# A two-layer encoder on one core: the attention's prologue in an order written by hand, pair 0's keys left unscaled, and x loaded into eight tiles of its own

## The chip, the cores and the metric

The kernel runs on one core of one Trainium2 chip. The metric is the device time of one execution in microseconds; a kernel's time is the median of several executions. The engines are named as in the profile: PE (matmuls), PEld (its weight loads), DVE, ACT, POOL, and SP, which here only issues transfers (DMAs).

## The reference, cut to what matters

The model has 512 tokens of width 1024 and two layers. Layer 0 mixes by stick-breaking attention (16 heads of 64), layer 1 by a gated linear recurrence; each is followed by an MLP with squared relu of width 4096, and a last RMS norm closes. All inputs and weights are float32. The change touches the attention and what is just behind it:

```python
h = rms_norm(x, norm_mix[0])
qkv = (h @ w_qkv).reshape(B, S, 3, 16, 64)
z = einsum('bhqd,bhkd->bhqk', q, k) * 64 ** -0.5        # per block of 128 queries
log_keep = where(mask, log_sigmoid(-z), 0)              # mask: k_pos < q_pos
after = reverse cumsum(log_keep) - log_keep
w = where(mask, exp(log_sigmoid(z) + after), 0)
o = einsum('bhqk,bhkd->bhqd', w, v)
x = x + o @ w_o
h = rms_norm(x, norm_mlp[0]);  u = relu(h @ w1);  x = x + (u * u) @ w2
```

## The kernel before, in words

**Layout.** x is held transposed, as 8 chunks of 128 channels by 512 tokens. A product of a weight with x is 8 steps over the chunks. Every float32 operand is cut into a high and a low half (`wh`, `wl` for weights: ACT casts the raw weights to the high half, L172, and DVE subtracts it from them, L173; `xgh`, `xgl` for x scaled by the norm's gain, `halves`, L110; `bh`, `bl` for the input of an output projection). One step is then three matmuls of 512 columns (`three`, L176 to L180). The RMS norm's factor depends on the token alone, so it is applied to the products: the sum of squares over the channels is gathered in one tile (ACT squares, POOL or DVE add).

**Who orders what.** Inside the attention the program order of PE is kept as written (`manual_schedule` for PE); the other engines' instructions, and SP's transfers, are put in order by the compiler's scheduler, from a simulated timeline. Every engine runs its own list in order, so an instruction that waits holds all that is behind it.

**The prologue (L267 to L303).** Ten warm-up matmuls run while the first data come. ACT's queue issues six fetches for the two weight slabs of pair 0 (q and k, each in parts of 2, 2 and 4 chunks), SP's queue the 8 chunks of x and the columns of gains. START is the order in which x chunks and slab parts are cut into halves, FIRST the order of the first 16 steps. The sum of squares is made by two chains of adds (even chunks on POOL, odd ones on DVE), which are added at L303.

**The norm (`inverse`, L305).** Four column sums on PE (L309, eight rows in the trace), a root on ACT, a reciprocal and the diagonal on DVE; then one product (L324) that spreads the factor over all partitions, as `r`. Its first part runs ahead of the filling steps, its second behind step BROAD = 4, and then pair 0's k is scaled with `r` and cut (`k_halves`, L247).

**The filling steps and the chains (L464 to L506).** The steps of the projections make up a list `fill`: for pair 1 its k, its q and the value projection of pairs 0 and 1, for pairs 2 to 7 k, q and half of a value projection (24 steps), at last the output projection: chunks 4 and 5 over their first 5 input chunks (EARLY; kept as `early`), chunks 0 to 3 over 7. Between them, at due times counted in filling steps, stand the steps of two chains of each pair p: 8 score steps from SCORE0 + PACE p (q times k into a bank `z`, two sigmoids on ACT, a mask on POOL, a scan on DVE, a product on POOL), and 17 value steps from VAL0 + PACE p (PE transposes the weights, L421, ACT and DVE cut them into `th` and `tl`, L434 and L435, PE multiplies with v; the last one writes `bh` and `bl` of the pair, L459 and L460).

To move halves of q and k to where the two heads need them, `stacked` (L226) issues four transfers for each of q, kh and kl. These read the tiles `xh` and `xl`, of which there is one each.

**Behind the chains (L509 to L542).** Chunks 0 to 3 get their last input chunk, the slabs of chunks 4 to 7 are loaded and cut, the 8 chunks of x are loaded anew into one tile `x`, POOL adds `early` to chunks 4 and 5, and `residual` finishes chunks 4 to 7, adds each chunk to x (L527), cuts it (L113, L114) and squares it for the next norm. The MLP's first product follows.

PSUM has eight banks, named by tags with two each: `acc`, `t`, `o`, `z`.

## Time and profile before

| | us |
|---|---|
| three executions | 1144.65, 1146.91, 1147.21 |
| median | 1146.91 |
| the profiled execution | 1143.47 |
| its span, first to last instruction | 1141.8 |
| attention and output projection, in that span | 0 to about 270 |

A profile shows one execution. A row of the timeline gives the start, the duration, the engine, the line, the operation and its operands, and in brackets how long the engine had been idle before it and what ended that. A row of the waits gives engine, line and what it waited for: the total, how often, the longest. Durations of single PE rows overlap, because matmuls are pipelined; what one costs is the distance of two starts.

### The profile page before, as it was taken

Reading aid. Unit: us, or ns where it says so; the run is one execution under the profiler, and the core shown is the slowest. Engines: PE = TensorE matmul, PEld = TensorE weight load, DVE = VectorE, ACT = ScalarE, POOL = GpSimd, SP = SyncE. Lnnn points to the kernel's source line nnn. Section 1 sums busy time; section 2 is a strip of 40 time slices with the busy share of each in tenths; the row PEclk is TensorE's granted clock in tenths of the full one; section 3 lists DMA queues with packets and bytes.
Section 4 is the critical chain, followed back from the end, with each engine's and each line's share of the span. In section 5 each row is a group of like instructions: output and inputs, shape, how many; then the busy total and the mean of one; then the engine's idle time right before and its main releaser. Section 6 shows DMA issues by size and latency. Waiting matters only on the chain.

```text
span 1141.8 us, 13730 instructions
## 1 busy us (share of the span) xinstructions
PE 1108.6 (97%) x5164; PEld 916.5 (80%) x5164; DVE 606.8 (53%) x741; ACT 464.9 (41%) x738; POOL 364.4 (32%) x328
## 2 busy tenths in 40 slices
PE   8899999989999999999999999799999999999997
PEld 6788888867888888888888788688888888888886
DVE  6477776738533443433464769855433433433513
ACT  6566666746322222221244457834222222222332
POOL 2345445425611520520543000422611511611520
PEclk9999999999999999999999999899999999999999
DMA  7544354316332332233232222122322332233401
GB/s 240 149 130 129 94 150 114 88 39 221 110 94 93 101 99 92 93 95 106 95 104 93 78 78 92 56 74 98 105 92 93 96 108 92 92 101 102 148 1 74
DMA packets 41154, 117.34 MB, mean 103 GB/s; under 512 B 7424, under 2 KB 8192, under 8 KB 41088
## 3 DMA queue, kind: packets, MB, share of 16 engines
q1 hardware_dynamic: 39904, 114.89, 32.4%
q10 hardware_dynamic: 1184, 1.57, 0.5%
q8 instruction: 41, 0.67, 0.3%
q14 instruction: 25, 0.20, 0.1%
HBM read 101.76 MB, written 2.10 MB: 91 GB/s over the span
## 4 chain that ended last, share of the span: by engine, by line
PE 86%; DVE 6%; ACT 4%; issue 2%; DMA 1%; POOL 1%; SPq 0%; ACTq 0%; DVEq 0%; POOLq 0%
PE ps_acc L178 10%; PE ps_acc L179 10%; PE ps_acc L180 10%; PE ps_t L179 7%; PE ps_t L178 7%; PE ps_t L180 7%; PE ps_o L179 7%; PE ps_o L180 7%; PE ps_o L178 7%; DVE wl L173 2%; PE ps_t L421 1%; PE ps_acc L342 1%; PE ps_acc L343 1%; PE ps_acc L344 1%; PE ps_o L443 1%
## 5 line engine op out<-in xcount | busy, mean ns | idle before, releaser
L172 ACT CAST wh<-raw 128x1024 fp32r<-128x1024 f32 (+3 forms) x206 | 185.7, 918 | 487.7 <-issue 217.8
L173 DVE TENSOR_TENSOR wl<-raw,wh 128x1024 fp32r<-128x1024 f32 (+3 forms) x206 | 259.6, 1272 | 61.2 <-ACT wh L172 60.3
L556 POOL TENSOR_TENSOR u<-t 128x512 f32<-128x512 f32 x64 | 66.5, 1041 | 403.9 <-DVE t L553 400.8
L178 PE MATMUL ps_acc<-xgh,wh 128*128 128x512 f32 x368 | 148.6, 404 | 0.8 <-ACT wh L155 0.8
L179 PE MATMUL ps_acc<-xgh,wl 128*128 128x512 f32 x368 | 146.0, 397 | 0.0
L180 PE MATMUL ps_acc<-xgl,wh 128*128 128x512 f32 x368 | 145.9, 396 | 0.0
L557 POOL TENSOR_TENSOR bl<-u,bh 128x512 fp32r<-128x512 f32 x64 | 131.4, 2054 | 8.6 <-issue 3.8
L178 PE MATMUL ps_t<-xgh,wh 128*128 128x512 f32 x224 | 88.3, 394 | 0.0
L179 PE MATMUL ps_t<-xgh,wl 128*128 128x512 f32 x224 | 88.0, 393 | 0.0
L180 PE MATMUL ps_t<-xgl,wh 128*128 128x512 f32 x224 | 87.7, 392 | 0.0
L180 PEld LDWEIGHTS ps_acc<-xgl,wh 128*128 128x128 f32 x368 | 70.2, 191 | 16.0 <-DVE xgl L114 0.4
L178 PEld LDWEIGHTS ps_acc<-xgh,wh 128*128 128x128 f32 x368 | 70.2, 191 | 14.9 <-ACT wh L155 1.1
L179 PEld LDWEIGHTS ps_acc<-xgh,wl 128*128 128x128 f32 x368 | 70.3, 191 | 13.3 <-DVE wl L156 0.5
L405 DVE TENSOR_TENSOR_SCAN scan<-keep,later 128x128 f32<-128x128 f32 (+1 forms) x64 | 60.1, 940 | 35.1 <-ACT keep L396 34.4
L178 PE MATMUL ps_acc<-bh,wh 128*128 128x512 f32 x190 | 75.0, 394 | 0.8 <-DVE x L527 0.8
L179 PE MATMUL ps_acc<-bh,wl 128*128 128x512 f32 x190 | 74.5, 392 | 0.0
L180 PE MATMUL ps_acc<-bl,wh 128*128 128x512 f32 x190 | 73.7, 391 | 0.0
L180 PE MATMUL ps_o<-xgl,wh 128*128 128x512 f32 x176 | 68.6, 391 | 1.0 <-DVE xgl L114 1.0
L179 PE MATMUL ps_o<-xgh,wl 128*128 128x512 f32 x176 | 69.5, 395 | 0.0
L178 PE MATMUL ps_t<-bh,wh 128*128 128x512 f32 x176 | 68.7, 391 | 0.5 <-ACT wh L172 0.5
L179 PE MATMUL ps_o<-bh,wl 128*128 128x512 f32 x176 | 69.2, 393 | 0.0
L178 PE MATMUL ps_o<-bh,wh 128*128 128x512 f32 x176 | 68.9, 391 | 0.0
(228 smaller groups left out, 2198.5 us busy)
## 6 DMA issues: line engine op xcount, KB each, us to landing
raw<-in_w_m SPq DMA_DIRECT2D x120, 512.0 KB, 3.5
raw<-in_w_in SPq DMA_DIRECT2D x16, 512.0 KB, 3.5
raw<-in_w_qk SPq DMA_DIRECT2D x14, 512.0 KB, 4.3
x<-in_xT SPq DMA_DIRECT2D x16, 256.0 KB, 5.7
raw<-in_w_v SPq DMA_DIRECT2D x8, 512.0 KB, 3.9
kl<-xl SPq DMA_DIRECT2D x32, 128.0 KB, 3.4
raw<-in_w_ro SPq DMA_DIRECT2D x8, 512.0 KB, 3.5
raw<-in_w_last SPq DMA_DIRECT2D x8, 512.0 KB, 4.2
```

What stands on the lines that cost most here:

```text
L172: A.copy(wh[:, k, :], raw[:, k, :])
L173: V.tensor_tensor(wl[:, k, :], raw[:, k, :], f(wh[:, k, :]), ALU.subtract)
L178: PE.matmul(ps, wh, ah, start=start, stop=False)
L179: PE.matmul(ps, wl, ah, start=False, stop=False)
L180: PE.matmul(ps, wh, al, start=False, stop=stop)
L342: PE.matmul(ps, xgh[:, k, ts], wh, start=k == 0, stop=False)
L343: PE.matmul(ps, xgh[:, k, ts], wl, start=False, stop=False)
L344: PE.matmul(ps, xgl[:, k, ts], wh, start=False, stop=k == C - 1)
L405: V.tensor_tensor_scan(sc[:, S - n : S][:, ::-1], keep[:, :n][:, ::-1], later[:, S - n :][:, ::-1], 1.0, ALU.mult, ALU.max,)
L421: PE.transpose(tr[:, (qb - kb) * P : (qb - kb + 1) * P], w[pair, j, qb][:, kb * P : (kb + 1) * P], ident,)
L556: G.tensor_tensor(u, t, t, ALU.mult)
L557: G.tensor_tensor(bl[:, c, :], u, f(bh[:, c, :]), ALU.subtract)
```

## The change

It does the following.

- **Prologue.** ACT, DVE, POOL and SP follow the program's order there. ACT's queue issues only four fetches, SP's queue the others: the last parts of q and k behind x chunk 4, then the slabs of pair 1 (`n`, `m`) and of the first value projection. START now lists the squares (`s`) and the cutting of `n` and `m` too. All eight squares have tiles of their own.
- **The norm.** Its two parts stand behind filling steps 4 (SUMS) and 8 (BROAD), with `high_priority` for ACT and DVE.
- **Pair 0.** Its k isn't scaled: both products are cut as soon as they are there (`first_halves`), and its scores are multiplied by `r` (DVE, PSUM to SBUF) before the sigmoids. All copies of it go out on SP's queue, head by head.
- **Pair 1** does q before k, from slabs cut in the prologue, in banks `t` and `o`. The first value slabs are cut behind the norm's root and its copy, and later slabs behind the copy.
- **Chains.** PACE is 23.7, VAL0 is 35, and the last pair's two chains span 4 steps less. The two sigmoids change places.
- **Output projection.** What is left of chunks 4 and 5 (3 input chunks, two of them here) and of 6 (7) are filling steps at the end of the list, with weight halves in tiles of the score halves (`late_slab`). Then each of chunks 0 to 6 gets its last input chunk.
- **x.** Eight tiles (`home`) hold the first x, then `keep`, `w3` and `osum`, and at last x again; seven of them are loaded when the late steps begin, where POOL adds `early` too.

Cut to its core:

```diff
 START = [
-    ("x", 0), ("q", 0), ("k", 0), ("x", 1), ("x", 2), ("q", 1), ("x", 3), ("k", 1),
-    ("x", 4), ("q", 2), ("x", 5), ("k", 2), ("x", 6), ("x", 7),
+    ("x", 0), ("q", 0), ("k", 0), ("s", 0), ("x", 1), ("q", 1), ("k", 1), ("x", 2), ("s", 1), ("x", 3),
+    ("s", 2), ("x", 4), ("q", 2), ("k", 2), ("x", 5), ("x", 6), ("x", 7), ("n", 0), ("n", 1), ("s", 3),
+    ("s", 4), ("s", 5), ("s", 6), ("s", 7), ("m", 0), ("m", 1),
 ]
-PACE = 24
+PACE = 23.7
-VAL0, VALS = 39, 21
-BROAD = 4
+VAL0, VALS = 35, 21
+LESS = 4
+SUMS = 4
+BROAD = 8
...
+    HOMES = (*(("keep", 4),) * 4, *(("w3", 3),) * 3, ("osum", 1))
...
+        def first_halves(pq, pk):
+            qh, ql = parted(pq, "x")
+            h = hp.tile([P, S], F32R, tag="th", name="th", bufs=3)
+            l = hp.tile([P, S], F32R, tag="tl", name="tl", bufs=3)
+            A.copy(h, pk)
+            V.tensor_tensor(l, pk, f(h), ALU.subtract)
+            q[0], kh[0], kl[0] = [], [], []
+            for j in range(2):
+                for tag, two, to in (("q", (qh, ql), q), ("kh", (h, h), kh), ("kl", (l, l), kl)):
+                    t = hp.tile([P, S], F32R, tag=f"{tag}{j}", name=f"{tag}{j}")
+                    for a, part in zip(half, two):
+                        nc.sync.dma_start(out=f(t[a, :]), in_=f(part[half[j], :]))
+                    to[0].append(t)
...
+        parts += [slab_parts(w, (0, 4, 8)) for w in (w_qk[0, 1], w_qk[1, 1], w_v[0, 0], w_v[0, 1])]
...
+        with tc.manual_schedule(engines=others):
+            for i in range(2):
+                for j in range(2):
+                    parts[j][2](i, A)
+            for c in range(C):
+                nc.sync.dma_start(out=xcs[c], in_=xT[:, c, :])
...
+                if c == 4:
+                    for j in range(2):
+                        parts[j][2](2)
+            for j in range(2, 6):
+                for i in range(2):
+                    parts[j][2](i)
+            for kind, c in START:
...
+                else:
+                    A.activation(sqs[c], xcs[c], AF.Square)
+                    if c > 1:
+                        e, acc = ((G, sums), (V, odd))[c % 2]
+                        e.tensor_tensor(acc, acc, sqs[c], ALU.add)
+            V.tensor_tensor(sums, sums, odd, ALU.add)
+            for i, k in FIRST:
+                xg_step(first[i], k, *parts[i][:2])
+            first_halves(*first)
...
+                    if pair == 0:
+                        V.tensor_tensor(keep[:, :n], z[:, :n], norm["r"][:, :n], ALU.mult)
+                        z = keep
+                    A.activation(wt, z[:, :n], AF.Sigmoid, scale=norm["rp"][:, qb : qb + 1])
                     A.activation(keep[:, :n], z[:, :n], AF.Sigmoid, scale=norm["rn"][:, qb : qb + 1])
-                    A.activation(wt, z[:, :n], AF.Sigmoid, scale=norm["rp"][:, qb : qb + 1])
...
+            if pair == 1:
+                return [
+                    (qk_steps(0, pair, q_halves, parts[2][:2], "t"), C),
+                    (qk_steps(1, pair, k_halves, parts[3][:2], "o"), C),
+                ]
...
+        LATE = sum(n for _, n in fill)
+        fill += [(so_late(4, "t", EARLY), 2), (so_late(5, "t", EARLY), 2), (so_late(6, "o", 0), C - 1)]
...
+            if i == LATE - 26:
+                late_slab(4, EARLY, ("kh0", "kl0"))
+                late_slab(5, EARLY, ("kh1", "kl1"))
+            if i == LATE - 14:
+                late_slab(6, 0, ("q0", "q1", "kh0", "kh1"))
+            if i == LATE:
+                x = [home_tile(tag, n, "x") for tag, n in HOMES[:7]]
+                for c in range(7):
+                    nc.sync.dma_start(out=x[c], in_=xT[:, c, :])
+                for c in early:
+                    G.tensor_tensor(x[c], x[c], early[c], ALU.add)
             next(steps)
-            if i == BROAD:
+            if i in (SUMS, BROAD):
                 next(inv)
...
+        for c in range(C - 1):
+            for _ in so_more(c, C - 1):
+                pass
+            if c == 0:
+                so_next = {C - 1: slab(w_so[C - 1], CUT)}
+        x.append(home_tile(*HOMES[7], "x"))
+        nc.sync.dma_start(out=x[7], in_=xT[:, 7, :])
```

More of the change, by code (lines that the diff above doesn't have):

```diff
@@ L255, in xg_step, with qk_steps @@
             three(ps, xgh[:, k, :], xgl[:, k, :], wh[:, k, :], wl[:, k, :], k == 0, k == C - 1)
-        def qk_steps(i, pair, then):
-            wh, wl = slab(w_qk[i, pair], CUT)
-            ps = bank("acc")
+        def qk_steps(i, pair, then, halves=None, tag="acc"):
+            if halves is None:
+                with tc.issue_after(norm["copy"].ins):
+                    halves = slab(w_qk[i, pair], CUT)
+            wh, wl = halves
+            ps = bank(tag)
             for k in range(C):
@@ L294, in hybrid_encoder @@
[L294 to L303 removed]
+        sums = work.tile([P, S], F32, tag="ssq", name="ssq", bufs=1)
+        odd = hp.tile([P, S], F32, tag="ks", name="odd", bufs=1)
```

156 lines of the change are left out of this document (78 added, 78 removed).

## The prediction

> **What bounds the kernel now.** I read the page first, for the share of each engine and the chain that ended last.
>
> ```profile
> span 1141.8 us, 13730 instructions
> PE 1108.6 (97%) x5164; PEld 916.5 (80%) x5164; DVE 606.8 (53%) x741; ACT 464.9 (41%) x738; POOL 364.4 (32%) x328
> PE 86%; DVE 6%; ACT 4%; issue 2%; DMA 1%; POOL 1%; SPq 0%; ACTq 0%; DVEq 0%; POOLq 0%
> ```
>
> The kernel is one long stream of matmuls. The change adds none and drops none (chunks 4 and 5 of the output projection still take 5 + 3 steps, chunk 6 still takes 8), so it can only gain time in which PE waits or runs slowly, or lose by new waits. Next come the stages, by windows of 20 us, and then PE's own waits up to the first MLP layer.
>
> ```profile
> 0.00:20.00 20.00, 18.06 (x68) 14.38 (x68) 12.85 (x20) 14.50 (x27) 6.53 (x18) 1.00 0.73 240
> 20.00:40.00 20.00, 14.95 (x53) 11.63 (x54) 10.39 (x22) 7.16 (x13) 0.04 (x1) 0.83 0.64 180
> 40.00:60.00 20.00, 18.55 (x131) 17.22 (x130) 13.48 (x19) 13.03 (x28) 10.82 (x16) 1.00 0.51 135
> ...
> 240.00:260.00 20.00, 15.87 (x76) 12.07 (x75) 10.55 (x21) 10.16 (x22) 2.90 (x2) 1.00 0.33 103
> ...
> 340.00:360.00 20.00, 20.00 (x88) 16.33 (x87) 6.97 (x7) 3.28 (x4) 0.00 (x0) 1.00 0.30 97
> ```
> ```profile
> PE ps_t L421 <- DVE tl L435: 4.8, 7, 0.8
> ...
> PE ps_z L309 <- DVE ssq L303: 3.7, 1, 3.7
> ...
> PE ps_acc L514 <- ACT bh L459: 2.0, 1, 2.0
> ...
> PE ps_acc L342 <- DVE v L350: 1.5, 1, 1.5
> ```
>
> Columns after the window: its length, then busy time of PE, PEld, DVE, ACT and POOL, PE clock, DMA share, GB/s. The last window is PE undisturbed: 20 us for 88 matmuls of 512 columns, **0.227 us each**; that is my price of a 512-column matmul (the 0.39 us of a single row overlaps its neighbours). Two windows fall short: 20 to 40 and 240 to 260. These are the two ends of the attention, and the change works on both.
>
> **The front, part by part.** These are rows of the timeline.
>
> ```profile
> 4.54 0.82 ACTq L151 DMA_DIRECT2D raw<-in_w_qk  x2
> 5.46 0.72 ACT L113 ACTIVATE xgh<-x,colt 128x512 fp32r<-128x512 f32 x1 [2.72 <-DMA raw<-in_w_qk]
> 6.53 0.79 PE L178 MATMUL ps_acc<-xgh,wh 128*128 128x512 f32 x1 [0.78 <-ACT wh L155]
> 19.61 0.39 PE L180 MATMUL ps_acc<-xgl,wh 128*128 128x512 f32 x1
> 23.64 1.47 PE L309 MATMUL ps_z<-ones,ssq 128*128 128x1 f32 x8 [3.65 <-DVE ssq L303]
> 24.98 0.77 PE L178 MATMUL ps_acc<-xgh,wh 128*128 128x512 f32 x1
> 31.26 1.02 PE L324 MATMUL ps_z<-diag,ones 128*128 128x512 f32 x2
> ```
> ```profile
> 24.98:31.20 6.22, 6.22 (x16) 4.92 (x17) 2.13 (x9) 0.26 (x1) 0.00 (x0) 0.52 0.82 244
> ```
>
> ```profile
> DMA to landing us min/median/max: 3.5/5.3/6.0
> ```
> ```profile
> 6.09 0.69 ACT L155 CAST wh<-raw 128x256 fp32r<-128x256 f32 x2
> ...
> 12.26 2.57 ACT L113 ACTIVATE xgh<-x,colt 128x512 fp32r<-128x512 f32 x4
> ...
> 15.25 1.14 ACT L172 CAST wh<-raw 128x512 fp32r<-128x512 f32 x2
> ```
> ```profile
> L135 POOL TENSOR_TENSOR ssq<-ssq,sq 128x512 f32<-128x512 f32 x10 | 16.5, 1647 | 25.7 <-ACT sq L134 25.5
> ```
>
> (a) *Start.* ACT's first scaling at 5.46 stands behind its own fifth and sixth weight fetch (4.54 to 5.36), which the change gives to SP, behind x chunk 4. The x chunks of the prologue take 3.5 us or more to land (first row), and the first and the columns are issued by about 1.3, so the scaling can begin at about 4.8: gain between 0 and 0.7, I take 0.6. From there ACT's new list is 8 scalings at 0.64 (2.57 / 4), 8 squares and 6 wide casts at 0.57 (1.14 / 2; I price a square like a cast) and 4 narrow casts at 0.35: 14.5 us, to 19.3. Only four squares, two casts and POOL's and DVE's adds stand behind what the first 48 matmuls need, so PE stays their bound. The sum of squares: square 6 at about 17.6, POOL's add 1.65, DVE's last add 0.7, so about 20.
>
> (b) *Gap.* The first pair ends at 19.61 + 0.23 = 19.84. PE then waits for the sum of squares, because its column sums (L309) stand ahead of all filling steps. In the new order they come behind five filling steps (SUMS is 4), 3.4 us later, at about 22.6, and the sum is there at 20. The eight small matmuls stay: 24.98 - 19.84 - 1.47 = **3.7 gained**. The cover is those five steps, whose weights (two slabs of pair 1) are in ACT's list ahead of the last squares; without them the wait is back whole.
>
> (c) *Half clock.* The 15 filling matmuls between 24.98 and 31.26 take 6.28 us where 15 x 0.227 = 3.4 would do; the window's granted clock is 0.52. It follows the idle gap, so it goes with it: **2.9 gained**.
>
> ```profile
> 35.03 2.95 SPq L232 DMA_DIRECT2D kl<-xl  x4
> 37.38 0.39 PE L180 MATMUL ps_acc<-xgl,wh 128*128 128x512 f32 x1
> 38.68 0.35 PE L392 MATMUL ps_z<-kh,q 128*128 128x256 f32 x1 [0.91 <-DMA kl<-xl]
> 39.72 0.39 PE L178 MATMUL ps_acc<-xgh,wh 128*128 128x512 f32 x1
> 45.48 0.40 PE L393 MATMUL ps_z<-kl,q 128*128 128x512 f32 x1
> 47.34 0.38 PE L342 MATMUL ps_acc<-wh,xgh 128*128 128x256 f32 x1 [1.45 <-DVE v L350]
> ```
>
> (d) *First scores.* Before, pair 0's k waits for the norm, and the copies of kl are issued at 35.03. PE's last filling matmul ends at 37.38 + 0.23 = 37.61 and the next begins at 39.72; two score matmuls of 256 columns (0.12 each) lie between: 1.9 us of waiting. In the change k isn't scaled; its halves are cut when the first pair ends (19.2 with (a)) and 12 copies go out on SP at 2.95 / 4 = 0.74 each or less. Those of the first head are issued by some 24 and land by 28; the first score step stands 13 filling steps behind 19.2, at 19.2 + 13 x 0.68 + 2 for the norm's matmuls = 30. **1.9 gained**, with two microseconds of cover; the cost if it fails is that wait again. What stays late is r, now needed by the first score instead: the root stands behind step 5 and the copy behind step 9, at about 27.5.
>
> (e) *Banks.* At 47.34 the value projection waited for its own eviction, held up on ACT behind pair 1's cast, 45.48 + 0.23 = 45.71 to 47.34: 1.6. The change gives pair 1's projections banks t and o, which no one else uses yet. **1.6 gained.**
>
> (f) *Added.* Pair 0's scores get eight DVE products from PSUM, which the trace of before lacks. The nearest rows are the same product for k and the other PSUM readers on DVE:
>
> ```profile
> L249 DVE TENSOR_TENSOR ks<-ps_acc,r 128x512 f32<-128x512 f32 x2 | 1.4, 687 | 5.8 <-ACT r L326 5.8
> ```
> ```profile
> L435 DVE TENSOR_TENSOR tl<-ps_t,th 128x384 fp32r<-128x384 f32 x16 | 8.7, 541 | 0.5 <-ACT th L434 0.5
> ...
> L435 DVE TENSOR_TENSOR tl<-ps_t,th 128x256 fp32r<-128x256 f32 x16 | 6.5, 404 | 0.3 <-ACT th L434 0.3
> ```
>
> With about 0.27 for 128 columns that is 2 x (0.69 + 0.54 + 0.40 + 0.27) = 3.8 us of DVE, less one k product (0.7). DVE was busy 10.4 + 13.5 us in the 40 us from 20 to 60; some 5.7 of it (adds, halves of pair 1's weights) moves ahead of 20, so 21 are left in the 29 us that remain. That is denser, 0.73 against 0.6, and the copies of pair 0 and of pair 1 queue on one SP while ACT's next cast waits for them (the tile is single). I bound new waits by 0 and by two or three like (e), 4: I take **1.5 lost**, near one of them, which is the one wait of that kind the trace has.
>
> **The middle.** The waits of the transposes for tl are 0.7 in every pair, when the third turn of a pair meets the next pair's k product and its weight halves on DVE. Values four steps earlier (35 for 39) put that third turn at 37.5, before k is done at step 40, and the pace of 23.7 moves it further off. Of 4.8 us I take **3.0 gained**. The bounds are 4.8 and a loss (below). Of the sigmoids' exchange: the scan starts up to 0.7 later and POOL's mask 0.7 earlier; nothing on PE waits for either within five steps, so nothing.
>
> **The tail.** From the last filling matmul to the first of the MLP:
>
> ```profile
> 243.70:270.36 26.66, 22.53 (x103) 17.61 (x102) 18.45 (x26) 17.02 (x30) 11.89 (x8) 1.00 0.47 158
> ```
> ```profile
> 276.27 0.50 PE L180 MATMUL ps_o<-xgl,wh 128*128 128x512 f32 x1 [1.04 <-DVE xgl L114]
> ```
>
> The work in it by the code: 80 matmuls of 512 columns (18 for chunks 4 and 5, 48 for 6 and 7, 12 to close 0 to 3, 2 values) x 0.227 = 18.2; four of 384 (0.17), eight of 256 (0.12), ten transposes (0.09): 2.5. So 20.7 of 26.7, and **6.0 is waiting**: on the last pair's chain (2.0 in one row), on x, which is loaded only after it, and on weight halves. In the new order the last transposes come by step 213 of 225, so 7 steps (4.8 us) of chunk 6 and then seven closing steps cover that chain; x is loaded at step 214 into tiles that are free by then. **6.0 gained.** Against it: DVE has eight adds, eight halves and three weight halves to do in the some 15 us from the last value to the MLP's eighth step, at 0.6 to 1.2 each, 12 to 17 us. So the wait at 276.27 (1.0) stays, and a new one lies between 0 and 2.5; I take **1.0 lost**. The loads of x and of the slabs 4 to 6 are no more bytes than before, they come earlier.
>
> **Sum.** 0.6 + 3.7 + 2.9 + 1.9 + 1.6 - 1.5 = 9.2 in the front, 3.0 in the middle, 6.0 - 1.0 = 5.0 in the tail: 17.2. The profiled execution took 1143.47 us (span 1141.8 and 1.7 around it), so it would be 1126.3. The median of the runs shown is 1146.91, 3.4 above it; with the same gain **1129.7, say 1130**. About 0.2% (2.3 us) is what a measurement of this kernel can tell from no change.
>
> **The rivals.**
>
> *As forecast*, 1130: chance 0.60.
>
> *New waits eat half of the front* (rival 1). ACT and SP follow a list by hand, so one late landing holds all behind it: if pair 1's second slab, whose buffer is free only when DVE has halved the first, comes after 19, then the cut of q and k, the root and the first scores move back with it. For it: the window 20 to 40 has a DMA share of 0.64 already. Against: 3.5 to 6 us of landing from 13 gives 17 to 19. PE would wait 2 to 4 at the first scores, and 2 to 4 for banks on DVE: 17.2 - 6 = 11, 1136. From a wait of about 3.4 us PE's clock would halve again, as in (c), for 3 more. Chance 0.20, with that of a tail that keeps its waits because x and the last slab come late (17.2 - 5 = 12, 1135).
>
> *The clock rises earlier* (rival 2). The start of before, too, runs at half speed:
>
> ```profile
> 1.12 4.63 PE L269 MATMUL ps_z<-ones 128*128 128x128 f32 x20 [1.12 <-DVE eps_t L100]
> ...
> 10.08 0.57 PE L179 MATMUL ps_acc<-xgh,wl 128*128 128x512 f32 x1
> ```
> ```profile
> 30.67 0.52 PE L179 MATMUL ps_acc<-xgh,wl 128*128 128x512 f32 x1
> ```
>
> The 0.57 at 10.08 is the first row under 0.63, as the 0.52 at 30.67 is at the end of (c): there the clock rises. Yet the warm-up matmuls had run from 1.12 to 5.75; between them and 6.53 lies 0.78 of idle time. With a start at 5.9 that hole nearly closes. If one unbroken busy stretch is what raises the clock, the six matmuls from 7.95 that stand 0.425 apart come 0.227 apart: 1.2 more, 1128.5. Chance 0.12. The Trainium skill, "TensorE: Matmul & The Clock Gate", Part 1, says that the activity window is about 3.4 us and free-running, so that a rise can come only at its ends; by that rule the rise here would come one window earlier or not at all. The trace agrees as far as it goes: its two rises, some 20.5 us apart, are six such windows.
>
> *Slower* (rival 3).
>
> ```profile
> L405 DVE TENSOR_TENSOR_SCAN scan<-keep,later 128x512 f32<-128x512 f32 x16 | 19.6, 1224 | 14.6 <-ACT keep L396 14.0 <-POOL w L409 0.7
> ```
>
> The value turns begin at 35 + 23.7 p and the next pair's scores at 35.7 + 23.7 p, so in every pair the turns share DVE with scans, 1.22 us for 512 columns. Should two turns of each pair find such a scan ahead of their tl while both t banks are full, that is 2.4 x 8 = 19.5 us against the 14.2 of the two ends, and the 3.0 of the middle is gone too: 1146.9 - 14.2 + 19.5 = 1152. It decides from 1.8 us a pair. For it: the 0.7 of before is a wait of this very kind. Against: turns are 1.24 steps apart with a product between from the third on, and DVE is busy under 0.8 in every window. Chance 0.06.
>
> *It does not do what it says*: the column sums still find an unfinished sum, because the lists on ACT and DVE run later than I add up; then (b) and (c) stay, 17.2 - 6.6 = 10.6, 1136. Chance 0.02.
>
> **Range and chances.** Low end: all waits of front and tail gone, the early clock and the whole middle, 17.2 + 1.5 + 1.0 + 1.2 + 1.8 = 22.7, 1124; high end: rival 1 with a tail that gains 2 less and no gain in the middle, 17.2 - 6 - 2 - 3 = 6.2, 1141. Outside lie rival 3 and the far ends of the others. Faster by over 0.2%: 0.92; the same: 0.03; slower: 0.05.
>
> **What would show it.** The first real matmul before 6.0; no wait for the sum of squares and a granted clock near 1.0 in 20 to 40; the first score step near 30 with no wait for a copy; the first chunk of the MLP some 17 us earlier than at 270.4. Fewer than seven waits of the transposes for tl would say that the middle is right. I am wrong if DVE is the releaser of PE's waits between 20 and 60, if a wait of over 3 us is left there, or if the last value's eviction or x still ends a wait at the tail.

## The result, and the profile after

The changed kernel takes **1132.29 us** in the median of four executions (1127.67 to 1134.89), the kernel before 1145.78 (1144.12 to 1147.21) on the same chip: a ratio of 0.9875, with a 95% interval of 0.9852 to 0.9898. On another chip it was 1129.65 against 1146.35, 0.9860 [0.9844, 0.9876]. The forecast was 1130, a gain of 17.2 us; 13.5 came on the first chip and 16.7 on the other. The four executions of the first chip differ by the granted clock of PE: its mean is 0.996 in the fastest, and 0.987 and 0.989 in the two that took over 1134 us. The profiled execution took 1129.96 us.

Its page, the lines for the span, the engines and the chain that ended last, and below them windows of 20 us (one of 25), with the same columns as before:

```profile
span 1128.2 us, 13701 instructions
PE 1102.7 (98%) x5164; PEld 914.1 (81%) x5164; DVE 605.3 (54%) x746; ACT 466.4 (41%) x736; POOL 362.1 (32%) x328
PE 88%; DVE 4%; ACT 4%; DMA 2%; issue 1%; SPq 0%; DVEq 0%; ACTq 0%
```
```profile
20.00:40.00 20.00, 19.03 (x112) 16.19 (x110) 13.93 (x29) 10.96 (x22) 2.48 (x6) 1.00 0.81 214
40.00:60.00 20.00, 17.35 (x107) 15.23 (x108) 18.20 (x29) 14.59 (x32) 10.62 (x16) 1.00 0.47 130
98.00:123.00 25.00, 22.91 (x124) 19.50 (x124) 20.25 (x31) 15.87 (x36) 9.99 (x16) 0.93 0.48 130
240.00:260.00 20.00, 20.00 (x90) 16.34 (x89) 11.90 (x17) 12.43 (x20) 6.48 (x4) 1.00 0.24 79
```

Both windows that fell short before, 20 to 40 and 240 to 260, are full now (PE 14.95 to 19.03 and 15.87 to 20.00), and the clock of the first is 1.00 for 0.83. The shortfall has moved: to 40 to 60, where PE's busy time is 17.35 for 18.55 and DVE is busy for 18.2 of 20, and to 98 to 123, where the clock is 0.93. PE's own waits say with what:

```profile
PE ps_t L501 <- DVE tl L515: 5.4, 4, 2.1
PE ps_acc L384 <- DVE v L392: 2.3, 1, 2.3
PE ps_z L343 <- DVE ssq L334: 0.8, 1, 0.8
```

The wait for the sum of squares is 0.8 instead of 3.7; the waits of the transposes for `tl` are four instead of seven, but 5.4 us instead of 4.8; and one wait for an eviction of v is still there, longer. Five rows of PE's timeline mark the road:

```profile
6.13 0.68 PE L181 MATMUL ps_acc<-xgh,wh 128*128 128x512 f32 x1 [0.38 <-ACT wh L158]
18.39 0.39 PE L181 MATMUL ps_t<-xgh,wh 128*128 128x512 f32 x1
30.13 0.28 PE L468 MATMUL ps_z<-kh,q 128*128 128x256 f32 x1
48.77 0.40 PE L181 MATMUL ps_acc<-xgh,wh 128*128 128x512 f32 x1
258.23 0.39 PE L181 MATMUL ps_acc<-xgh,wh 128*128 128x512 f32 x1
```

They are the first real matmul (6.53 before), the first step of pair 1, which is the end of pair 0's projections (19.84 before), the first score (38.68 before), the first step of pair 2 (57.29 before) and the first of the MLP (270.37 before). So the front gained **8.5**, what lies between pair 2's first step and the MLP went from 213.1 to 209.5, **3.6**, and behind the MLP's first step another 1.5 came: 13.6 of span in all.

### The profile page after: what moved, and what is told of

Same layout as the page of the kernel before. It is cut to its first block, busy times and chain, and to the rows that moved or that the text cites. A ratio compares the mean times of both kernels' runs of the same rounds, so it can differ in the third digit from the quotient of the medians.

```text
span 1128.2 us, 13701 instructions
## 1 busy us (share of the span) xinstructions
PE 1102.7 (98%) x5164; PEld 914.1 (81%) x5164; DVE 605.3 (54%) x746; ACT 466.4 (41%) x736; POOL 362.1 (32%) x328
## 4 chain that ended last, share of the span: by engine, by line
PE 88%; DVE 4%; ACT 4%; DMA 2%; issue 1%; SPq 0%; DVEq 0%; ACTq 0%
PE ps_acc L181 10%; PE ps_acc L182 10%; PE ps_acc L183 10%; PE ps_t L182 8%; PE ps_t L181 8%; PE ps_t L183 8%; PE ps_o L182 7%; PE ps_o L181 7%; PE ps_o L183 7%; DVE wl L176 1%; PE ps_t L501 1%; DMA raw<-in_w_qk 1%; PE ps_o L523 1%; PE ps_o L522 1%; PE ps_z L469 1%
## 5 line engine op out<-in xcount | busy, mean ns | idle before, releaser
L175 ACT CAST wh<-raw 128x1024 fp32r<-128x1024 f32 (+2 forms) x192 | 179.0, 946 | 496.2 <-issue 203.8
L176 DVE TENSOR_TENSOR wl<-raw,wh 128x1024 fp32r<-128x1024 f32 (+2 forms) x192 | 246.6, 1295 | 58.5 <-ACT wh L175 58.1
L181 PE MATMUL ps_acc<-xgh,wh 128*128 128x512 f32 x344 | 137.3, 399 | 0.4 <-ACT wh L158 0.4
L182 PE MATMUL ps_acc<-xgh,wl 128*128 128x512 f32 x344 | 135.3, 393 | 0.1
L183 PE MATMUL ps_acc<-xgl,wh 128*128 128x512 f32 x344 | 134.9, 392 | 0.1
L181 PE MATMUL ps_t<-xgh,wh 128*128 128x512 f32 x248 | 98.3, 397 | 0.0
L182 PE MATMUL ps_t<-xgh,wl 128*128 128x512 f32 x248 | 97.4, 393 | 0.0
L183 PE MATMUL ps_t<-xgl,wh 128*128 128x512 f32 x248 | 97.0, 391 | 0.0
L489 POOL TENSOR_TENSOR w<-w,scan 128x128 f32<-128x128 f32 (+1 forms) x64 | 54.6, 854 | 57.4 <-DVE scan L485 56.1
L181 PE MATMUL ps_o<-xgh,wh 128*128 128x512 f32 x176 | 69.5, 395 | 0.0
```

Source lines behind the costliest of these rows:

```text
L175: A.copy(wh[:, k, :], raw[:, k, :])
L176: V.tensor_tensor(wl[:, k, :], raw[:, k, :], f(wh[:, k, :]), ALU.subtract)
L181: PE.matmul(ps, wh, ah, start=start, stop=False)
L182: PE.matmul(ps, wl, ah, start=False, stop=False)
L183: PE.matmul(ps, wh, al, start=False, stop=stop)
L489: G.tensor_tensor(wt, wt, sc[:, S - n + 1 : S + 1], ALU.mult)
```

## The experiments

Twelve kernels ran, each beside the kernel before on the same chip. Given are the median, the ratio to the kernel before and its 95% interval; the changed kernel's are 0.9875 and 0.9860, above.

Differences of two or three microseconds between two such kernels need care. Behind some 570 us, where no edit changes anything, the changed kernel's two traces have 6.83 us at half clock; others have up to 17.07, and their last 2400 matmuls take 554.6 to 554.9 us instead of 551.5. So I also compare where one and the same matmul begins, the 2400th from the end of 5164 ("mark" from here on): at 583.81 in the kernel before, at 570.27 and 569.93 in the changed kernel's two traces. That is one trace each, and it still holds the half clock of the part ahead of it.

### Front: the column sums

*Column sums first.* One edit puts them ahead of the filling steps again:

```diff
         inv = inverse()
+        next(inv)
         steps = chain(*(g for g, _ in fill))
...
-            if i in (SUMS, BROAD):
+            if i == BROAD:
```

> The column sums stand ahead of all filling steps again, as before; the prologue by hand and the rest stay. Theory (the place behind five steps is what hides the sum of squares): PE idles from 18.4 to about 22.7 and the clock halves, 5 to 8 us more than the changed kernel, some 1138. Rival (the hand order alone makes the sum early enough, or later waits hide it): 0 to 2 us more.

Measured: 1131.75 us, 0.9897 [0.9877, 0.9918], two to four microseconds over the changed kernel by the ratios. PE's timeline:

```profile
23.09 1.46 PE L343 MATMUL ps_z<-ones,ssq 128*128 128x1 f32 x8 [4.04 <-DVE ssq L334]
...
24.99 0.63 PE L182 MATMUL ps_t<-xgh,wl 128*128 128x512 f32 x1
...
29.68 0.63 PE L181 MATMUL ps_t<-xgh,wh 128*128 128x512 f32 x1
```

The wait of 4.0 us and the half clock behind it (matmuls 0.63 long, 0.43 apart) are back whole, as steps (b) and (c) said, so both belong to the place of the column sums. Together they are some 6 us. The medians show a third to two thirds of that, with intervals that overlap the changed kernel's; the mark is at 574.37, 4.1 and 4.4 later. The wait of 2.3 us at 42 isn't in this trace: PE, arriving later, finds v evicted. So later waits hide a part, as the rival says; the size lies between its 0 to 2 and the theory's 5 to 8.

### Front: the unscaled k

*Pair 0's k scaled by r again*, its `kh` copies on ScalarE's queue, no products in the scores:

```diff
-            first_halves(*first)
+            q_halves(0, first[0])
...
             norm["r"] = r
+            k_halves(0, first[1])
...
-                    if pair == 0:
-                        V.tensor_tensor(keep[:, :n], z[:, :n], norm["r"][:, :n], ALU.mult)
-                        z = keep
```

> Of the changed kernel, pair 0's k is again scaled by r ahead of its split, with its kh copies on ScalarE's queue, and the eight products by r in the scores of pair 0 are gone. Theory (the unscaled k lets the scores start without the chain of the sums, and the products cost little): the first score waits 4 to 5 us near 30 us for its stacked k, the wait at 42.15 goes, and the time is 2 us (0 to 4) longer than the changed kernel's. Rival (the eight products and the long run of copies cost as much as they win): the time is the same or up to 2 us shorter.

Measured: 1138.87 us, 0.9952 [0.9935, 0.9970]: 9 to 10 us slower than the changed kernel by the ratios, with the mark at 578.60, 8.3 and 8.7 later. Theory and rival were both far too low. PE's timeline, and below it SP's:

```profile
40.22 0.55 PE L469 MATMUL ps_z<-kh,q 128*128 128x256 f32 x1 [10.36 <-DMA kl<-xl]
```
```profile
32.75 7.08 SPq L242 DMA_DIRECT2D kl<-xl  x4
```

PE reached the first score at 29.9 and stood **10.4 us** for the copies of kl: they stand on SP behind pair 1's q and three slab loads, and they couldn't be issued before the tiles `xh` and `xl`, of which there is one each, were free of pair 1's q. All that the earlier steps of the prologue had gained is given back in this one wait; the first score comes at 40.22, later than the 38.68 of before. So the value of the unscaled k is no longer the wait that stood there before, 1.9, but the 10 us that the other edits would have turned into it. That holds for SP's list in the order that it has here; what the scaled k would cost with pair 0's copies ahead of pair 1's, no run shows.

### Front: the wait at 42 us

In the changed kernel PE stands 2.35 us for v at 42.15. ACT's timeline shows what held v up:

```profile
42.15 0.35 PE L384 MATMUL ps_acc<-wh,xgh 128*128 128x256 f32 x1 [2.35 <-DVE v L392]
```
```profile
35.59 1.14 ACT L175 CAST wh<-raw 128x512 fp32r<-128x512 f32 x2 [2.21 <-DMA raw<-in_w_qk]
...
38.93 0.62 ACT L250 CAST xh<-ks 128x512 fp32r<-128x512 f32 x1 [0.89 <-DMA q<-xh]
```

ACT runs its list in order. It waits for a slab of pair 2 and then, at pair 1's k, for the copies that still read `xh`; the sigmoids and the evictions of v stand behind both. Two causes were possible: SP issues too late, or the DMA engines move too slowly.

*kh on ScalarE's queue*, which takes four of SP's twelve copies away:

```diff
-                        nc.sync.dma_start(out=f(t[a, :]), in_=f(part[half[j], :]))
+                        (A if tag == "kh" else nc.sync).dma_start(out=f(t[a, :]), in_=f(part[half[j], :]))
```

> One edit of the changed kernel: the four copies of pair 0's kh go on ScalarE's queue, as before the change; those of q and kl stay on SyncE's. Theory (SyncE's queue): the slab load of the values that follows stands behind twelve copies, which SyncE issues from 20.2 to 31.4 us; with eight copies it is issued about 3.7 us earlier, ScalarE's 2.21 us wait for it at 35.6 goes, and TensorE's 2.35 us wait at 42.15 shrinks to under 1 us: 1.5 to 2.5 us less than the changed kernel's 1129 to 1132. Rival (VectorE's products of pair 0's scores make the sigmoids late): the wait at 42 stays at 2 us or more and the time stays within 1 us.

Measured: 1131.30 us, 0.9879 [0.9858, 0.9899], no gain. The slab load was issued at 28.26 instead of 31.43, and ACT's wait for it is gone, as the theory of SP's queue has it. But:

```profile
38.09 0.62 ACT L250 CAST xh<-ks 128x512 fp32r<-128x512 f32 x1 [3.58 <-DMA q<-xh]
```
```profile
42.13 0.35 PE L384 MATMUL ps_acc<-wh,xgh 128*128 128x256 f32 x1 [2.51 <-DVE v L392]
```

The wait only went on to the next transfer: q's copies, issued at 30.5, now land beside three slabs, and ACT waits 3.58 us for them. The theory of the queue fell. The rival, VectorE's products, isn't named by any of these rows either, so I formed a third.

*Loads held.* Pair 2's q slab and the value slabs of pairs 2 and 3 are issued behind the last copy of pair 1 (pair 2's k slab behind pair 1's q copies):

```diff
-                with tc.issue_after(norm["copy"].ins):
+                with tc.issue_after(norm["copy"].ins), tc.issue_after(norm["kl" if i == 0 or pair > 2 else "q", 1].ins):
                     halves = slab(w_qk[i, pair], CUT)
...
-                ws = [slab(w_v[m, i], CUT) for i in range(2)]
+                with tc.issue_after(norm["kl", 1].ins):
+                    ws = [slab(w_v[m, i], CUT) for i in range(2)]
```

> One edit of the changed kernel: on SyncE's queue the load of pair 2's q slab and the two value slabs of pairs 2 and 3 stand behind the last kl copy of pair 1, so that 1.5 MB less goes through the DMA engines between 24 and 44 us, where they were busy for 0.94 of the time. Theory (the DMA engines are the bound of the first 45 us: the copies of pair 1's q land late, ScalarE's cast of its k waits for them, and the sigmoids and the evictions of v behind that cast come late): ScalarE's waits of 2.21 and 0.89 us shrink below 0.5, TensorE's 2.35 us wait at 42.15 to under 1 us, and the time is 1 to 3 us less than the changed kernel's. Rival (the wait at 42 is owed to the order of ScalarE's and VectorE's own work): it stays at 2 us or more, and the time is the same or longer, since the held slabs come late for pair 2.

Measured: 1129.32 us, 0.9853 [0.9830, 0.9875]; the changed kernel beside it 1129.65, 0.9860 [0.9844, 0.9876]. The windows of the changed kernel and of this one (share of the DMA engines and GB/s are the last two columns), and this one's waits of PE:

```profile
24.00:44.00 20.00, 17.65 (x110) 15.54 (x109) 14.00 (x30) 12.90 (x25) 4.86 (x9) 1.00 0.94 251
```
```profile
24.00:44.00 20.00, 19.61 (x125) 17.46 (x124) 15.42 (x31) 13.09 (x25) 6.47 (x11) 1.00 0.86 215
```
```profile
PE ps_t L504 <- DVE tl L518: 6.8, 4, 2.1
...
PE ps_acc L387 <- DVE v L395: 0.4, 1, 0.4
```

The mechanism is as expected: with fewer bytes on the way the wait for v is 0.4 us, and pair 2's first step comes at 46.90, where the changed kernel's two traces have 48.77 and 50.48. The time doesn't show it: the wait for `tl` at 53.87 grew from 0.50 to 1.65, DVE's list there being what it was, and the MLP's first step, at 256.19, is only 1.7 and 2.0 us earlier than in those two (257.89 and 258.23). Of that the profiled execution keeps nothing: it has 13.65 us at half clock behind the mark instead of 6.83. The front's new wait is owed to the **transfers** (the copies of pair 1's q landed 2.3 us after their issue, in the median, where it was 5.8), and a good part of its removal is given back at the next bound, DVE. One thing the run doesn't separate: ACT's list has pair 1's cast ahead of the slab's here, and behind it in the changed kernel.

### Middle

The wait of 2.09 us at 104.55, in DVE's and PE's timelines of the changed kernel:

```profile
101.54 2.36 DVE L176 TENSOR_TENSOR wl<-raw,wh 128x512 fp32r<-128x512 f32 x2
103.82 0.68 DVE L515 TENSOR_TENSOR tl<-ps_t,th 128x512 fp32r<-128x512 f32 x1
```
```profile
104.55 0.44 PE L501 MATMUL ps_t<-ident,w 128*128 128x128 f32 x2 [2.09 <-DVE tl L515]
...
105.93 0.63 PE L181 MATMUL ps_acc<-xgh,wh 128*128 128x512 f32 x1
...
108.49 0.61 PE L182 MATMUL ps_acc<-xgh,wl 128*128 128x512 f32 x1
```

The third turn's `tl` stands on DVE behind two low halves of a value slab. Value slabs are cut once in two pairs, and the waits lie at 54.58, 104.55, 155.63 (the third turns of pairs 0, 2 and 4) and at 205.43 (pair 6, where slabs of the output projection take their place). Behind one of them the clock is halved for seven matmuls.

*Value slabs behind tl.*

```diff
-                ws = [slab(w_v[m, i], CUT) for i in range(2)]
+                with tc.issue_after(norm["tl", 0, 2].ins): ws = [slab(w_v[m, i], CUT) for i in range(2)]
...
-                V.tensor_tensor(dl, tr[:, :n], f(dh), ALU.subtract)
+                norm["tl", j, kb] = V.tensor_tensor(dl, tr[:, :n], f(dh), ALU.subtract)
```

> The value slabs' halves of pairs 2, 4 and 6 are put behind the third turn's tl on DVE, nothing else changes. Theory (these halves ahead of tl make three of the four waits in the middle): the waits near 55, 105 and 156 go, 3.5 us, and the slow clock behind the second, 1.5 us: 3 to 5 us less than the changed kernel. Rival (DVE is simply full there, the wait goes to the next turn or to weights): within 1.5 us of the changed kernel, with PE waiting for another releaser.

Measured: 1127.20 us, 0.9842 [0.9821, 0.9863], two to four microseconds under the changed kernel, with the mark at 566.02, 3.9 and 4.3 earlier: the theory holds. PE's waits keep one of the four, the one of pair 6, which the edit doesn't touch:

```profile
PE ps_t L501 <- DVE tl L515: 2.1, 1, 2.1
```

*The old pace* (24 and 39, with the last pair's values capped so that they end where the late steps need them):

```diff
-PACE = 23.7
+PACE = 24
-VAL0, VALS = 35, 21
+VAL0, VALS = 39, 21
```

> PACE 24 and VAL0 39 as before, all else as changed (the last pair's values begin at 200.9 as in the changed kernel, or x would be loaded ahead of its last transposes). Theory (the four waits for tl come from weight halves of the value slabs that stand ahead on DVE, every other pair, and the new value start moved the turns onto them): those 5.4 us of waits and the slow clock behind one of them give way to the seven waits of 0.7 of before, 0 to 3 us less than the changed kernel. The prediction's step (the new start takes the turns away from k's product): 3 us more.

Measured: 1135.28 us, 0.9921 [0.9905, 0.9937], five to seven microseconds slower than the changed kernel. The new pace and value start do gain, so the forecast's reason for the middle had the right sign; what went wrong is beside it. In the changed kernel the old pace doesn't bring back the 4.8 us of waits of before, but more. The waits of PE with it:

```profile
PE ps_t L501 <- DVE tl L515: 5.8, 6, 1.1
...
PE ps_o L523 <- DVE lastl L515: 2.2, 3, 0.8
```

*The kept share's sigmoid first*, from pair 1 on, as before the change:

```diff
-                    A.activation(wt, z[:, :n], AF.Sigmoid, scale=norm["rp"][:, qb : qb + 1])
-                    A.activation(keep[:, :n], z[:, :n], AF.Sigmoid, scale=norm["rn"][:, qb : qb + 1])
+                    first_out = [(wt, "rp"), (keep[:, :n], "rn")]
+                    for t, s in first_out if pair == 0 else first_out[::-1]:
+                        A.activation(t, z[:, :n], AF.Sigmoid, scale=norm[s][:, qb : qb + 1])
```

> One edit of the changed kernel: for the pairs from 1 on, the sigmoid of the kept share is issued ahead of that of the weight, as before the change. Theory of the prediction (the exchange of the two sigmoids is worth nothing, since TensorE waits for neither): time within 1 us of the changed kernel's. Rival (the weight first lets GpSimd's selects and VectorE's scans start some 0.6 us earlier, which is what keeps the third turns' tl on time): the waits for tl, 5.4 us in four turns, grow by 2 to 4 us, and the time with them.

Measured: 1129.45 us, 0.9860 [0.9843, 0.9877], not to be told from the changed kernel by the time; the mark is at 568.07, 1.9 and 2.2 earlier. The rival had the sign wrong: PE's waits for `tl` fell.

```profile
PE ps_t L502 <- DVE tl L516: 3.2, 3, 1.8
```

### Tail

*No late steps.* Chunks 4 to 6 are finished behind the chains as before; x stays in its eight tiles:

```diff
-        fill += [(so_late(4, "t", EARLY), 2), (so_late(5, "t", EARLY), 2), (so_late(6, "o", 0), C - 1)]
...
-            if i == LATE - 26:
-                late_slab(4, EARLY, ("kh0", "kl0"))
-                late_slab(5, EARLY, ("kh1", "kl1"))
-            if i == LATE - 14:
-                late_slab(6, 0, ("q0", "q1", "kh0", "kh1"))
```

> The changed kernel without the late steps: chunks 4 to 6 are finished behind the chains as before, x is still loaded into its eight tiles as soon as they are free. Theory (the late steps cover the last pair's chain): the waits of the tail come back, on the last bh, on weight halves and on x, 5 to 8 us more than the changed kernel, some 1138. Rival (what counted in the tail was the early load of x): 1 to 2.5 us more, 1134.

Measured: 1132.25 us, 0.9893 [0.9874, 0.9912], two to four microseconds over the changed kernel, with intervals that overlap, and the mark at 573.57, 3.3 and 3.6 later: under the theory's 5 to 8, a little over the rival's 1 to 2.5. The tails' waits, without the late steps and then in the changed kernel, between 200 and 275 us:

```profile
PE ps_acc L605 <- ACT bh L539: 2.0, 1, 2.0
PE ps_t L501 <- DVE tl L515: 0.5, 1, 0.5
PE ps_o L183 <- DVE xgl L117: 0.3, 1, 0.3
```
```profile
PE ps_t L501 <- DVE tl L515: 1.9, 1, 1.9
```

The wait for the last pair's `bh` is the late steps' to hide, and comes back without them, at 241.39, with 3.41 us at half clock behind it. The waits for x and for weight halves, which before the change stood behind it, do not. For x that is the early load into tiles of its own: it is issued from 215.28 on here, and was from 251.53 before. For the weight halves no run shows the reason. And the late steps charge for their gain: halves of their slabs (1.29 us at 199.01) stand on DVE ahead of those that `tl` waits for at 205.43, and that wait is 1.86 with them and 0.47 without.

### Put together

*Four edits*: value slabs and output-projection slabs behind `tl`, `kh` on ScalarE's queue, and the final sum of squares ahead of pair 1's k halves.

```diff
+            with tc.issue_after(norm["tl", 0, 2].ins):
-            wh, wl = slab(w_so[c], CUT)
+                wh, wl = slab(w_so[c], CUT)
...
+                    if (kind, c) == ("m", 0):
+                        V.tensor_tensor(sums, sums, odd, ALU.add)
```

> Four edits of the changed kernel together: the halves of the value slabs stand behind the third turn's tl (as in the run that measured 1127.2), those of the output-projection slabs too, kh's copies of pair 0 go on ScalarE's queue, and the final sum of the squares stands ahead of the two slab halves that came before it on VectorE. Theory (each removes a wait of its own: 3.8 measured for the first, 1.9 at 205.43 for the second, 1.5 to 2.5 at 42.15 for the third, 0.8 at 22.72 for the fourth): 1123 to 1126 us in the median. Rival (a later wait or the end of the chain takes over, since work that is moved back is late for its own readers): 1127 or more, no better than the first edit alone.

Measured: 1128.78 us, 0.9854 [0.9838, 0.9869], no better than the first edit alone; the rival holds (the mark is at 567.63, the first edit's at 566.02). PE's waits:

```profile
PE ps_acc L385 <- DVE v L393: 3.0, 1, 3.0
...
PE ps_acc L182 <- DVE wl L176: 1.6, 1, 1.6
```

The wait for the sum of squares is gone and that at 42 has grown; the slabs that no longer hold `tl` at 205 are late for their own matmuls instead.

*Value slabs behind tl, kept share first:*

> Two edits of the changed kernel that were measured one by one: the halves of the value slabs behind the third turn's tl, and the sigmoid of the kept share first again from pair 1 on. Theory (both act on the same waits, those for tl in the even pairs: with the first edit only the wait near 200 us was left, with the second 3.2 of 5.4 us): the gains do not add; 1125.5 to 1128, at most 1.5 us below the first edit alone (1127.2). Rival (they act on different waits): 1122 to 1125.

*The same, with the loads held:*

> Three edits of the changed kernel together: the value slabs' halves behind tl, the kept share's sigmoid first from pair 1 on, and the three slab loads held behind pair 1's copies. Theory (the DMA engines bound the first 45 us): 1 to 3 us less than the run with the first two edits alone, 1123 to 1126. Rival (the held loads win nothing, or make the value slabs late): no less than that run.

*The changed kernel beside them:*

> The changed kernel itself, on the chip of the three runs of this call, so that their single edits are compared with it on the same chip. Expected by all theories: 1129 to 1133, a ratio between 0.985 and 0.990 to the kernel before; the wait near 42 us and those for tl as in the first profile, while the half-clock stretch after one of them may lie elsewhere, as it has in the other runs.

Measured on one chip:

| | median, us | ratio to before | 95% interval | mark, us |
|---|---|---|---|---|
| changed kernel | 1129.65 | 0.9860 | 0.9844 to 0.9876 | 569.93 |
| loads held | 1129.32 | 0.9853 | 0.9830 to 0.9875 | 568.23 |
| value slabs behind `tl`, kept share first | 1124.25 | 0.9817 | 0.9793 to 0.9842 | 565.58 |
| all three | 1123.53 | 0.9802 | 0.9786 to 0.9819 | 562.16 |

The pair of edits has its median in the rival's range, the edits adding up, while the interval reaches into the theory's. Its waits for `tl` are 1.1 in all, where the first edit alone left 2.1 and the second 3.2: the same waits, but not the same part of them. With the loads held as well the median is 0.7 us lower, less than the intervals can tell, so its theory isn't settled by the time; the mark is 3.4 earlier, of which about half is a stretch of 3.41 us at half clock that the pair's trace has at 43 and this one hasn't. Its span, and two lines of PE's waits:

```profile
span 1121.5 us, 13723 instructions
```
```profile
PE ps_t L505 <- DVE tl L519: 1.4, 2, 1.1
...
PE ps_acc L387 <- DVE v L395: 0.7, 1, 0.7
```

Of the wait at 42, 0.75 us is left (at 40.08), and between the start and the mark no stretch is at half clock. The changed kernel came out as expected, its half-clock stretch elsewhere than in the first trace. All three edits together are the best version here: some 6 us under the changed kernel, about 23 under the kernel before.

## Why the prediction came out as it did

**The front: 9.2 forecast, 8.5 measured.** Nearly right in the sum, less so in its terms, and in part by luck: the clock gave 1.05 that the sum doesn't hold.

(a) and rival 2: the first matmul came 0.40 earlier (0.6 forecast), the first pair's end 1.45. The other 1.05 is the clock, which rose at 6.55 instead of 10.46; that is nearly the 1.2 of rival 2, to which I had given 0.12. The trace of the loads held, where it rose at 10.57, shows the price: its first pair ends at 19.49, 1.1 later. The reason that I gave is borne out in part only: a hole counts, but where it falls is chance (see the last section).

(b) and (c): the gap went, but for a 0.78 wait that I hadn't foreseen. DVE's list has the low halves of pair 1's k ahead of the final sum, which is done at 22.7 instead of my 20. The half clock behind the gap went whole. The run with the column sums first shows that both are as large as forecast, and that by the medians a third to two thirds of them hide under a later wait.

(d) The score waits for no copy, as forecast, but the two microseconds of cover were not there: the first head's copies were issued until 26.5, not 24, and those of kl landed 4.2 us after their issue in the median, so near 30, for a score at 30.13. Its size was wrong by its meaning: I priced the wait that stood in the trace of before, 1.9. Once the steps ahead of it are faster, the same copies are worth 10.4, as the run with k scaled shows. (b) and (c) could be cashed only because of (d).

(e) This term gained nothing. The second block of values found a bank free, as forecast, but the third waits for the eviction of the first, because the values take only the two banks `acc`: 2.35 at 42.15, where 1.45 stood at 47.34 before. The banks of pair 1 were not what held the eviction; ACT's list was.

(f) The new waits were forecast at 1.5, between 0 and 4. By the sum, which has 1.6 for (e), they are 2.35 + 0.78 = 3.1, twice the forecast and within its bounds. The place was right (copies of two pairs, ACT's cast waiting for the single `xh`), the culprit half: not SP's queue of issues, as I had it, but the DMA engines at a share of 0.94.

**The middle: +3.0 forecast, between -2 and -3 measured. This is the step that failed**: "put that third turn at 37.5, before k is done at step 40". It left the k product, as I said, and the old pace costs five to seven microseconds. But I moved one instruction past one neighbour and did not list the others on its engine: once in two pairs the third turn now meets a value slab, whose two low halves take 2.36 us on DVE. The waits went from 4.8 to 5.4 (0.6 of the 4.8, at 246.07, was in the tail), and a half-clock stretch of about 1.5 came with them (seven matmuls 0.43 apart that would be 0.227). The run with the value slabs behind `tl` shows the cause: three of the four waits go, and the mark is 3.9 to 4.3 us earlier. I had named the half clock as something that follows a wait of about 3.4; here it followed 2.1. The exchange of the sigmoids, which I priced at nothing, accounts for some of it by the waits (5.4 against 3.2), though not measurably by the time alone.

**The tail: 5.0 forecast, 7 to 8 measured.** The 3.6 between pair 2's first step and the MLP, and the 2 to 3 lost in the middle, make about 6 gained, which is the "6.0" of the forecast; PE has no wait there from 206 us on. No row measures middle and tail apart: the split rests on the waits and the half clock of the middle. The 1.0 that I took off for a dense DVE is the term that was mis-sized: the wait at 276.27 is gone too, so it is 1.0 gained for 1.0 lost. That the tail's surplus makes up for part of the middle's loss is luck too. What the profile of the tail couldn't say is that the gain has two owners: the late steps for the wait on `bh`, x's early load for the waits on x.

**Rival 1** came true in its mechanism (a landing that holds ACT's list) and not in its size; its clock penalty fell elsewhere. **Rival 3** was the right engine and the right instruction, `tl` on DVE, with the wrong blocker: slab halves in every second pair, not scans in every pair. That is why it cost 2 to 3 and not 19. The first score at 30 came out (30.13), the copies that "are issued by some 24 and land by 28" came two microseconds later.

**The signs that I had named.** The first matmul before 6.0: no, 6.13. No wait for the sum of squares: no, 0.78. The clock at 1.00 in 20 to 40 and the first score near 30: yes. The MLP 17 us earlier: 12.1. Fewer than seven waits for `tl` was a bad sign for the middle: they are four, and longer in sum. DVE as the releaser of PE between 20 and 60 was to say that I am wrong, and it is what ends both the wait at 42 and the one at 54.58.

Open: how the 5.1 us that middle and tail gained together (3.6 and 1.5) divide between the two to better than a microsecond, and what the unscaled k is worth with another order of SP's copies.

## What to carry to other kernels

Price the removal of a wait by what would arrive there once everything ahead of it is faster, not by its length in the trace of before: here 1.9 us became 10.4. When an instruction is moved along an engine's list, write down every neighbour that it may meet over a whole period (here two pairs), not only the one that it leaves. And when several transfers end a stage's waits in turn, look at the share of the DMA engines before moving issues from queue to queue. Before two kernels that differ by 2 or 3 us are ranked, compare the start of one and the same matmul and the time at half clock.

## What the runs showed of the hardware

**Half clock after short waits.** Stretches in which matmuls took twice their time followed waits of PE of about 2 us in some executions and not in others of the same program. Of seven traces with a wait of 2.3 to 2.6 us near 42, five have the stretch behind it and two haven't. In the changed kernel's first trace it came after the 2.09 us at 104.55 and not after the 2.35 us at 42.15; in its second trace it is the other way round. Windows of the first trace, then of the second (the clock is the third column from the end):

```profile
102.13:105.54 3.41, 1.32 (x8) 0.86 (x7) 3.20 (x6) 1.38 (x5) 2.33 (x3) 1.00 0.46 154
105.54:108.95 3.41, 3.41 (x11) 2.73 (x10) 1.06 (x2) 0.84 (x2) 0.94 (x2) 0.50 0.31 118
```
```profile
40.45:43.86 3.41, 1.51 (x13) 1.54 (x14) 3.41 (x6) 2.56 (x6) 2.43 (x3) 1.00 0.99 282
43.86:47.27 3.41, 3.41 (x18) 3.41 (x17) 2.71 (x6) 1.63 (x3) 2.94 (x5) 0.50 0.61 136
```

Both stretches last 3.41 us. The others in the fourteen traces, but for the one in which each trace ends, last as long, or two or three times as long: 6.83 in the trace of before (24.11 to 30.94, the stretch of (c)), 10.24 with k scaled (34.98 to 45.22). In the second trace the stretch begins 1.5 us after PE is back at work. So the start isn't tied to the end of the wait. It is tied to a grid: steps of 3.41 us, counted from where the clock first rises (6.55 in the first trace, 6.31 in the second), end where each stretch begins.

This grid tells which waits halve the clock, because only the part of a wait that lies within one step counts. In the first trace the 2.09 us lie whole within 102.13 to 105.54, while the 2.35 us at 42.15 are split at 40.69 into 0.89 and 1.46. In the second the 2.43 us at 42.35 have 1.90 in one step, and the wait of 2.09 us that ends at 105.54 has 1.85 in one and 0.24 in the next. In the first 250 us of the fourteen traces, once the clock had risen, half clock followed every step with 1.90 us or more of waiting and none with 1.85 or less. Later, behind 600 us, the bound is less sharp: 1.62 us without a matmul sufficed once, and 1.89 once did not. Where the grid lies differs from execution to execution, and that is why the same wait costs some 1.5 us in one and nothing in the next.

The Trainium skill, "TensorE: Matmul & The Clock Gate", Part 1, describes such a grid: a free-running window of about 3.4 us. The length agrees. The same part says that the clock falls after at least one idle window; here 1.90 us of waiting in one sufficed, little more than half of it, and the measurement decides.

At the start it is alike. With k scaled the clock rose at 4.26, ahead of a hole of 0.68 us between warm-up and first matmul. In the changed kernel's first trace it rose at 6.55, at the end of a step that held the hole of 0.38. With the loads held a hole of 0.54, and in the trace of before one of 0.78, lay in a step that ended without a rise (at 7.16 and 7.05), and the clock rose one step later. So the hole of rival 2 matters where it falls into such a step, and where the steps end is chance.

**DVE beside POOL.** A low half of 512 columns took 1.18 us at 101.54 (2.36 for two, in the row above) while POOL was at work. With the value slabs behind `tl`, four of the same came at 102.76, when POOL ran for 0.41 and 0.33 us only:

```profile
102.76 2.58 DVE L176 TENSOR_TENSOR wl<-raw,wh 128x512 fp32r<-128x512 f32 x4
```

That is 0.65 each; POOL's rows in the changed kernel:

```profile
101.83 1.52 POOL L540 TENSOR_TENSOR bl<-osum,bh 128x512 fp32r<-128x512 f32 x1 [1.99 <-ACT bh L539]
103.30 0.75 POOL L479 TENSOR_SCALAR_AFFINE_SELECT w<-w 128x128 f32<-128x128 f32 x1
```

The Trainium skill, "SBUF — State Buffer", "SBUF: two separate sides", says that a VectorE instruction with two SBUF inputs and a GpSimd instruction that reads SBUF lock a shared port against each other for a whole instruction; these rows agree. By them the slab halves ahead of `tl` take nearly twice the 0.65.
